# Even layer in parity order: tokens stay sorted by parity up to the heads' outputs

## The chip, the cores and the metric

One Trainium2 chip; the program runs on one of its cores. The metric is the device time of one execution in microseconds (us), as the median over several runs. The profiled execution is a run of its own, and its trace gives the start and length of every instruction on TensorE (PE for matmuls, PEld for its weight loads), VectorE (DVE), ScalarE (ACT), GpSimd (POOL) and on the DMA queues.

## The reference, cut to what matters

A two-layer encoder over 256 tokens of width 2048. The even layer projects the normalised input to two groups of heads: A, eight heads of dilated window attention with three dilations each, and B, four heads of differential attention. The dilations are 1, 4 and 16, so keys of the two wider groups always have the parity of the query's token.

```python
def even_mixer(y, w_in, w_out, ...):
    proj = jnp.einsum("bsd,de->bse", y, w_in)
    pa = proj[..., :a_cols].reshape(b, s, A_GROUPS, 3, A_HEADS, HEAD_DIM)
    for gi, (window, dilation) in enumerate(((128, 1), (512, 4), (2048, 16))):
        o, lse = dilated_window_attention(pa[:, :, gi, 0], pa[:, :, gi, 1], pa[:, :, gi, 2], cols, window, dilation)
    out_a = jnp.sum(softmax(lses) * outs)
    o_b = differential_attention(q_b, k_b, v_b, t5_table[:, 24:], lam)
    o_b = rmsnorm(o_b, subln) * (1.0 - lambda_init)
    return jnp.einsum("bse,ed->bsd", concat(out_a, out_b), w_out)

def reference(x, ...):
    for layer in range(2):
        h = h + (even_mixer if layer % 2 == 0 else odd_mixer)(rmsnorm(h, ln_mix[layer]), ...)
        h = h + conv_ffn(rmsnorm(h, ln_ffn[layer]), ...)
    return rmsnorm(h, ln_final)
```

## The kernel before

All weights stream from HBM in units of 128 x 1024 fp32 (`wunit`, DMAs on SP's queue). Each unit is split into two fp32r parts: ScalarE casts the high part (`wh`), VectorE subtracts to get the low part (`wl`). Activations are held the same way, as two parts of 128 features x 256 tokens (`yT`). A product of two such numbers takes three partial products.

Two kinds of projection exist. `gemm_b` makes features x tokens (used for q and k): the weights are the stationary operand and all 256 tokens stream past. `gemm_a` makes tokens x features (used for V and for output projections): 128 tokens of `yT` are the stationary operand and 512 columns of weights stream past. `gemm_a` with 16 feature tiles has 8 units, and a unit has 2 feature tiles x 2 token blocks x 3 partial products = 12 matmuls. In the A heads, the V products of the two wider dilations (g = 1 and 2) pass `strided=True`: their token blocks are all even and all odd tokens, read out of natural order with a step of two.

The row factor 1 / rms of the layer norm isn't applied to `yT`; it is applied to the products. `row_factor` gives `rstd` (tokens on partitions). `row_broadcast` spreads it to `R` (tokens along the free axis): VectorE copies each half to a 128 x 128 tile `rb`, two TensorE transposes put them into a PSUM tile, VectorE copies that to `R`. Then two more TensorE transposes of `R`, read with a step of two, give `rstd_par`: the factors of the even and of the odd tokens on partitions (lines 390 to 401). `v_tiles` scales a V product by `rstd` or `rstd_par` while it copies it out of PSUM: ScalarE the high part, VectorE then the low part.

The PSUM pool has four tiles with the tag `gm`; each `gemm_a` takes two. So the third `gemm_a` can start only when `v_tiles` has read the first. The first V product of a head group runs ahead of `row_factor`, the second too (`v_ps`).

For q and k, `halves` multiplies by `Rq` or `R` and writes the tokens in parity order and reversed (q of A), in parity order (k of the wider groups), reversed (q of B) or plainly. `a_local` and `b_logits` add the bias to the logits through `bias_view`. `a_values` and the transposes of B's probabilities bring the tokens back to natural order.

The order of work is that of the program's text, with a small list of pending work (`later`, `tick`): softmax, transposes and value products of one head run some projections later. A scheduler then sets each engine's own order; engines run theirs strictly in order and wait for one another by semaphores.

Of the kernel before, what the change touches and what calls it, by code (L numbers as in the profile page):

```python
# [54 lines left out]
def trunk_kernel(ctx: ExitStack, tc, a, out):  # L58
# [13 lines left out]
    def nm(s):  # L72
        uid[0] += 1
        return f"{s}_{uid[0]}"
# [61 lines left out]
        tick()  # L136
        return ps

    def a_unit(ps, src, u, act, nk, strided=False, parts=1):
        last = 2 * u + 2 == nk  # L140
        a_products(ps, wunit(src[u], parts), u, act, nk, strided,
                   [(t, k) for t in range(2) for k in range(2)] if last else
                   [(t, k) for k in range(2) for t in range(2)])

    def a_products(ps, w, u, act, nk, strided, order):
        wh, wl = w
        for t, k in order:
            kt = u * 2 + k
            sl = slice(k * 512, (k + 1) * 512)
            if strided:  # L150
                ah, al = (act[kt][:, x, :].rearrange("p (j r) -> p r j", r=2)[:, t, :] for x in range(2))
            else:
                ah, al = (act[kt][:, x, t * P:(t + 1) * P] for x in range(2))
            T.matmul(ps[t], ah, wh[:, sl], start=(kt == 0), stop=False)  # L154
            T.matmul(ps[t], ah, wl[:, sl], start=False, stop=False)  # L155
            T.matmul(ps[t], al, wh[:, sl], start=False, stop=(kt == nk - 1))  # L156

    def gemm_a(src, act, nk, strided=False, hooks={}, first=1):

        ps = [tps("gm", 4), tps("gm", 4)]  # L160
        for u in range(nk // 2):
            if u in hooks:
                hooks[u]()
            a_unit(ps, src, u, act, nk, strided, parts=1 if u else first)
            if u % 2 == 1:
                tick()
        return ps

    def natural(ap):
        return ap.rearrange("p (a b) -> p a b", b=2)  # L170
# [9 lines left out]
    def halves(ps, r, order=None):  # L180

        t0 = tmp.tile([P, SEQ], F32, name=nm("t0"), tag="t0")
        S.copy(t0, ps[:, 0, :])  # L183
        V.tensor_tensor(t0, t0, ps[:, 1, :], op=ALU.add)  # L184
        t2 = tmp.tile([P, SEQ], F32, name=nm("t2"), tag="t2")
        if order in (parity, parity_rev):
            V.tensor_tensor(order(t2), natural(t0), natural(r), op=ALU.mult)
        else:
            V.tensor_tensor(order(t2) if order else t2, t0, r, op=ALU.mult)
        return t2  # L190

    def split(dst_h, dst_l, src):
# [47 lines left out]
    def row_factor():  # L240
        ss = tmp.tile([P, 2], F32, name=nm("ss"), tag="ss")
        V.tensor_reduce(ss, ssq_now[0], axis=AX.X, op=ALU.add)
        return rsqrt_mean(ss, D, "rstd", const)

    def row_broadcast(rstd):

        ps = tps("tp", 2)
        for t in range(2):
            b = tmp.tile([P, P], F32, name=nm("rb"), tag="rb")
            V.tensor_copy(b, rstd[:, t:t + 1].to_broadcast([P, P]))  # L250
            T.transpose(ps[:, t * P:(t + 1) * P], b, ident)
        r = const.tile([P, SEQ], F32, name=nm("R"), tag="R", bufs=1)
        V.tensor_copy(r, ps[:, 0:SEQ])
        return r

    def query_factor(R):
# [51 lines left out]
    def logits(q, k):  # L308
        ps = two(tps("s", 2))
        for t in range(2):  # L310
            qh = q[:, 0, t * P:(t + 1) * P]
            ql = q[:, 1, t * P:(t + 1) * P]
            T.matmul(ps[:, t, :], qh, k[:, 0, :], start=True, stop=False)  # L313
            T.matmul(ps[:, t, :], qh, k[:, 1, :], start=False, stop=False)  # L314
            T.matmul(ps[:, t, :], ql, k[:, 0, :], start=False, stop=True)  # L315
        return ps

    def bias_view(b, step):

# [58 lines left out]
    def x_rows(c):  # L378
# [8 lines left out]
    bmask = load("bmask", (28, NREL), pool=tmp, tag="ry", eng=nc.sync)  # L387
    onehot2 = load("onehot2", (32, 256), pool=tmp, tag="rx", eng=nc.sync)
    bmask2 = load("bmask2", (16, 256), pool=tmp, tag="ry", eng=nc.sync)
    v_ps.append(gemm_a(a["eva_v"][1], yT, KT, strided=True,  # L390
                       hooks={u: lambda u=u: x_rows(u) for u in range(4)}))
    for c in range(4):
        squares(c)
    rstd = row_factor()
    R = row_broadcast(rstd)
    Rq = query_factor(R)
    rstd_par = const.tile([P, 2], F32, name="rstd_par")
    ps = two(tps("tp", 2))
    for t in range(2):
        T.transpose(ps[:, t, 0:P], R.rearrange("p (j r) -> p r j", r=2)[:, t, :], ident)  # L400
    V.tensor_copy(rstd_par, ps[:, :, 0])

    rel = dram.tile([28, NREL + 1], F32, name="rel")
# [13 lines left out]
    def new_sc():  # L417
        return att.tile([P, 2, 512], F32, name=nm("sc"), tag="sc", bufs=1)

    def a_bias(hd, g):  # L420
        if g:
            b = att.tile([P, P], F32, name=nm("bias2"), tag="bias2", bufs=2)
            G.dma_start(b, bass.AP(tensor=rel2.tensor, offset=rel2.offset + ((g - 1) * 8 + hd) * 256,
                                   ap=[[1, P], [1, P]]))
            return b
        b = att.tile([P, 384], F32, name=nm("bias"), tag="bias", bufs=2)
        G.dma_start(b[:, 0:257], bass.AP(tensor=rel.tensor, offset=rel.offset + hd * (NREL + 1),
                                         ap=[[2, P], [1, 257]]))
        return b

    def a_local(q, k, b, sc):
        sc.append(new_sc())
        sc = sc[0]
        V.tensor_tensor(sc[:, :, 0:SEQ], logits(q, k), bias_view(b, 1), op=ALU.add)

    def a_strided(g, q, k, b, sc):

# [45 lines left out]
    def a_head(hd, vg):  # L483
        sc = []
        for g in range(3):
            b = a_bias(hd, g)
            q = qk_tile(a["eva_qk"][hd * 6 + 2 * g], yT, Rq, parity_rev, 2 * g)
            k = qk_tile(a["eva_qk"][hd * 6 + 2 * g + 1], yT, R, parity if g else None, 2 * g + 1)
            if g == 0:
                later(2, lambda q=q, k=k, b=b: a_local(q, k, b, sc))  # L490
            else:
                later(2, lambda g=g, q=q, k=k, b=b: a_strided(g, q, k, b, sc))

        def soft():
            softmax(sc[0])
            later(2, lambda: a_transposes(sc[0], hd, vg), 1)
        later(2, soft)

    for hh in range(2):
        vg = []  # L500
        for g in range(3):
            ps = v_ps.pop(0) if v_ps else gemm_a(a["eva_v"][hh * 3 + g], yT, KT, strided=(g > 0))
            if hh and g == 0:
                flush()
            vg.append(v_tiles(ps, rstd_par if g else rstd, range(8 + 4 * g, 12 + 4 * g)))
        for hd in range(hh * 4, hh * 4 + 4):
            a_head(hd, vg)

# [15 lines left out]
    def b_logits(m, q, k, sc, bias):  # L524
        if m == 0:
            sc.append(new_sc())
        V.tensor_tensor(sc[0][:, :, m * SEQ:(m + 1) * SEQ], logits(q, k), bias_view(bias, P), op=ALU.add)

    def b_softmax(hd, sc, vt):
        w = sc[0].rearrange("p t (m k) -> p t m k", m=2)  # L530
# [14 lines left out]
        later(2, lambda: b_transposes(hd, w, vt), 1)  # L545

    def b_transposes(hd, w, vt):
        pt = transposed_probs(w[:, 0, 0, :], w[:, 1, 0, :], rev)
        later(1, lambda: b_values(hd, pt, vt), 0)

    def b_values(hd, pt, vt):
# [19 lines left out]
    def b_finish(hd, o):  # L571
        ps = two(tps("tp", 2))
        for f in range(2):
            for t in range(2):
                T.transpose(ps[:, f, t * P:(t + 1) * P], o[:, t, f * P:(f + 1) * P], ident)
            y = new_act("mix", 8 + 2 * hd + f)
            split_scaled(y[:, 0, :], y[:, 1, :], ps[:, f, :], sub_gain[:, f:f + 1])
            mix[8 + 2 * hd + f] = y

    for pair in range(2):  # L580
        vt = v_tiles(gemm_a(a["evb_v"][pair], yT, KT), rstd, range(20 - 4 * pair, 24 - 4 * pair))
        for hd in (2 * pair, 2 * pair + 1):
            bias = att.tile([P, 384], F32, name=nm("bias"), tag="bias", bufs=2)
            G.dma_start(bias, bass.AP(tensor=rel.tensor, offset=rel.offset + (24 + hd) * (NREL + 1),
                                      ap=[[1, P], [1, 384]]))
            sc = []
            for m in range(2):
                q = qk_tile(a["evb_qk"][hd * 4 + m], yT, Rq, rev, 2 * m)
                k = qk_tile(a["evb_qk"][hd * 4 + 2 + m], yT, R, None, 2 * m + 1)
                later(2, lambda m=m, q=q, k=k, sc=sc, bias=bias: b_logits(m, q, k, sc, bias))  # L590
            later(2, lambda hd=hd, sc=sc, vt=vt: b_softmax(hd, sc, vt))
# [187 lines left out]
    def finish_all(src, act, y):  # L779
# [12 lines left out]
        kept = [(u, wunit(src[3][u])) for u in range(nu - AHEAD, nu)]  # L792
        for t in range(2):
            for u, w in kept:
                a_products(ps, w, u, act, HALF_F, False, [(t, 0), (t, 1)])
            finish_rows(t, ps[t])

    ffn(1, yT, None, last=True)
# [50 lines left out]
def _arrays(i):  # L849
    i = {k: np.asarray(v) for k, v in i.items()}  # L850
    r = {}
    r["x"] = i["x"].reshape(SEQ, D)
    r["xT"] = i["x"].reshape(SEQ, 8, 2, P).transpose(1, 3, 2, 0).reshape(8, P, 2 * SEQ)
    r["ln"] = np.stack([i["ln_mix"], i["ln_ffn"]]).reshape(4, KT, P).transpose(2, 0, 1)
    r["lnf"] = i["ln_final"]
    r["t5"] = i["t5_table"]
# [47 lines left out]
```

## Time and profile before

| | |
|---|---|
| median of 3 runs | 2485.79 us (2485.61 to 2485.87) |
| the profiled execution | 2485.5 us |
| its span, first to last instruction | 2483.7 us |
| TensorE matmuls busy | 2472.6 us |
| VectorE busy | 1671.2 us |
| ScalarE busy | 1227.8 us |
| DMA, mean rate | 187 GB/s |

The span leaves 1.8 us of the execution outside of it. Busy time of TensorE counts a matmul from its issue to its modelled end, so consecutive matmuls overlap; the step between their starts tells the pace. The A heads run until some 440 us, the B heads until some 585 us, the even layer's output projection follows, then the first FFN and the odd layer.

### The profile page before, as it was taken

The numbers are of one execution on the slowest core, as the hardware profiler recorded it, in microseconds if no ns is written. First come the engines' busy times: TensorE is split into PE (matmuls) and PEld (weight loads), VectorE is DVE, ScalarE is ACT, GpSimd is POOL, SyncE is SP. The second block draws the span as 40 slices with busy tenths as digits, with TensorE's granted clock in tenths as the row PEclk, the third lists the DMA queues.
The fourth block names the chain that finished last, engine by engine and source line by source line (L and its number), as shares of the span: only waits on it lengthen the run. The fifth ranks groups of instructions, "written<-read, shape, count | busy, mean of one in ns | idle before, by whom it ended". The sixth has DMA issues, their size and how long they took to land.

```text
span 2483.7 us, 34336 instructions
## 1 busy us (share of the span) xinstructions
PE 2472.6 (100%) x13115; PEld 2124.2 (86%) x13115; DVE 1671.2 (67%) x2454; ACT 1227.8 (49%) x1853; POOL 45.7 (2%) x71
## 2 busy tenths in 40 slices
PE   9999999999999999999999999999999999999998
PEld 7888888888888888888888888888888888888887
DVE  6677577676577775477775568765777755777754
ACT  6454445465554443344444457545544433444443
POOL 0000000001000000000000000100000000000000
PEclk9999999999999999999999999999999999999999
DMA  8655555556555555566655555765565655655654
GB/s 290 198 170 180 182 180 182 181 181 176 175 188 188 187 188 193 193 189 189 190 185 190 187 186 164 174 175 180 186 192 187 188 191 193 192 188 188 191 188 144
DMA packets 129951, 463.86 MB, mean 187 GB/s; under 512 B 15216, under 2 KB 15340, under 8 KB 129786
## 3 DMA queue, kind: packets, MB, share of 16 engines
q1 hardware_dynamic: 127018, 455.31, 57.1%
q0 software_dynamic: 2624, 6.32, 2.3%
q8 instruction: 102, 1.67, 0.3%
q14 instruction: 63, 0.52, 0.1%
q10 hardware_dynamic: 144, 0.03, 0.0%
HBM read 459.44 MB, written 2.17 MB: 186 GB/s over the span
## 4 chain that ended last, share of the span: by engine, by line
PE 99%; DMA 0%; DVE 0%; ACT 0%; SPq 0%; issue 0%; DVEq 0%; ACTq 0%
PE gm L126 38%; PE gm L129 20%; PE gm L155 13%; PE gm L154 13%; PE gm L156 13%; PE tp L330 0%; PE tp L237 0%; PE s L313 0%; PE s L315 0%; PE s L314 0%; DMA raw<-in_eva_v 0%; PE s L474 0%; PE s L443 0%; PE s L467 0%; PE s L342 0%; PE s L341 0%
## 5 line engine op out<-in xcount | busy, mean ns | idle before, releaser
L194 DVE TENSOR_TENSOR wl<-raw,wh 128x1024 fp32r<-128x1024 f32 (+1 forms) x857 | 1049.0, 1225 | 723.8 <-ACT wh L193 719.4
L193 ACT CAST wh<-raw 128x1024 fp32r<-128x1024 f32 (+1 forms) x857 | 898.6, 1049 | 1146.4 <-issue 501.8
L126 PE MATMUL gm<-yT,wh 128*128 128x512 f32 x4096 | 1029.1, 393 | 0.0
L126 PEld LDWEIGHTS gm<-yT,wh 128*128 128x128 f32 x4096 | 736.5, 189 | 132.6 <-DVE yT L200 0.7
L129 PEld LDWEIGHTS gm<-yT,wl 128*128 128x128 f32 x4096 | 558.7, 190 | 39.8
L129 PE MATMUL gm<-yT,wl 128*128 128x256 f32 x4096 | 571.2, 282 | 0.0
L154 PE MATMUL gm<-wh,prod 128*128 128x512 f32 x704 | 274.5, 390 | 0.0
L156 PE MATMUL gm<-wh,prod 128*128 128x512 f32 x704 | 274.3, 390 | 0.0
L155 PE MATMUL gm<-wl,prod 128*128 128x512 f32 x704 | 274.0, 389 | 0.0
L155 PE MATMUL gm<-wl,yT 128*128 128x512 f32 x416 | 163.4, 393 | 0.5 <-DVE wl L194 0.5
L154 PE MATMUL gm<-wh,yT 128*128 128x512 f32 x416 | 163.3, 395 | 0.5 <-ACT wh L193 0.5
L156 PE MATMUL gm<-wh,yT 128*128 128x512 f32 x416 | 163.0, 392 | 0.0
L156 PEld LDWEIGHTS gm<-wh,prod 128*128 128x128 f32 x704 | 132.2, 188 | 27.4
L155 PEld LDWEIGHTS gm<-wl,prod 128*128 128x128 f32 x704 | 132.2, 188 | 27.1
L154 PEld LDWEIGHTS gm<-wh,prod 128*128 128x128 f32 x704 | 132.2, 188 | 27.0
L184 DVE TENSOR_TENSOR t<-t,gm 128x256 f32<-128x256 f32 x256 | 105.9, 414 | 0.0
L154 PE MATMUL gm<-wh,mix 128*128 128x512 f32 x256 | 101.0, 394 | 0.0
L155 PE MATMUL gm<-wl,mix 128*128 128x512 f32 x256 | 100.4, 392 | 0.0
L156 PE MATMUL gm<-wh,mix 128*128 128x512 f32 x256 | 100.3, 393 | 0.0
L155 PEld LDWEIGHTS gm<-wl,yT 128*128 128x128 f32 x416 | 78.9, 190 | 17.3 <-DVE wl L194 1.4
L154 PEld LDWEIGHTS gm<-wh,yT 128*128 128x128 f32 x416 | 78.6, 190 | 17.5 <-ACT wh L193 1.4
L183 ACT COPY t<-gm 128x256 f32<-128x256 f32 x256 | 92.9, 363 | 0.0
(206 smaller groups left out, 1506.7 us busy)
## 6 DMA issues: line engine op xcount, KB each, us to landing
raw<-in_up SPq DMA_DIRECT2D x352, 512.0 KB, 4.3
raw<-in_down SPq DMA_DIRECT2D x176, 512.0 KB, 3.4
raw<-in_eva_qk SPq DMA_DIRECT2D x96, 512.0 KB, 3.5
raw<-in_eva_v SPq DMA_DIRECT2D x47, 512.0 KB, 3.5
raw<-in_evb_qk SPq DMA_DIRECT2D x32, 512.0 KB, 3.3
raw<-in_ev_out SPq DMA_DIRECT2D x32, 512.0 KB, 3.5
raw<-in_od_qk SPq DMA_DIRECT2D x32, 512.0 KB, 3.5
raw<-in_od_out SPq DMA_DIRECT2D x32, 512.0 KB, 3.4
```

Source lines behind the costliest of these rows:

```text
L126: T.matmul(flat, wh[:, sl], y.rearrange("p a b -> p (a b)"), start=(u == 0 and k == 0), stop=False)
L129: T.matmul(ps[:, 1, :], wl[:, sl], y[:, 0, :], start=False, stop=(u * 8 + k == KT - 1))
L154: T.matmul(ps[t], ah, wh[:, sl], start=(kt == 0), stop=False)
L155: T.matmul(ps[t], ah, wl[:, sl], start=False, stop=False)
L156: T.matmul(ps[t], al, wh[:, sl], start=False, stop=(kt == nk - 1))
L183: S.copy(t0, ps[:, 0, :])
L184: V.tensor_tensor(t0, t0, ps[:, 1, :], op=ALU.add)
L193: S.copy(dst_h, src)
L194: V.tensor_tensor(dst_l, src, dst_h.bitcast(F32), op=ALU.subtract)
```

## The change

The tokens of the even layer are put in parity order (all even tokens, then all odd ones) on the host, in `xT`. Thus `yT` is in parity order, and every `gemm_a` reads plain runs of 128 tokens; the `strided` form goes. `row_broadcast` writes the first layer's `R` in parity order, `rstd_par` is transposed from plain halves of it, and all V products of the even layer are scaled by `rstd_par` (before, A's g = 0 and both of B were scaled by `rstd`). q is only reversed and k is written plainly. The biases of A's g = 0 and of B come from one loader, `row_bias` (rows that step by two, 257 columns), and are added through the stepped view `parity_bias`. B's outputs go back to natural order where they leave PSUM in `b_finish`. The weights, the products and their number stay.

```diff
-    def a_products(ps, w, u, act, nk, strided, order):
+    def a_products(ps, w, u, act, nk, order):
...
-            if strided:
-                ah, al = (act[kt][:, x, :].rearrange("p (j r) -> p r j", r=2)[:, t, :] for x in range(2))
-            else:
-                ah, al = (act[kt][:, x, t * P:(t + 1) * P] for x in range(2))
+            ah, al = (act[kt][:, x, t * P:(t + 1) * P] for x in range(2))
...
-        if order in (parity, parity_rev):
-            V.tensor_tensor(order(t2), natural(t0), natural(r), op=ALU.mult)
-        else:
-            V.tensor_tensor(order(t2) if order else t2, t0, r, op=ALU.mult)
+        V.tensor_tensor(order(t2) if order else t2, t0, r, op=ALU.mult)
...
-        V.tensor_copy(r, ps[:, 0:SEQ])
+        if by_parity:
+            V.tensor_copy(parity(r), natural(ps[:, 0:SEQ]))
+        else:
+            V.tensor_copy(r, ps[:, 0:SEQ])
...
+    def parity_bias(b):
+
+        return bass.AP(tensor=b.tensor, offset=b.offset, ap=[list(b.ap[0]), [1, 2], [1, 2], [2, P]])
+
+    def by_parity(ap):
+        return ap.rearrange("p t (b a) -> p t b a", b=2)
...
-    R = row_broadcast(rstd)
+    R = row_broadcast(row_factor(), by_parity=True)
...
-        T.transpose(ps[:, t, 0:P], R.rearrange("p (j r) -> p r j", r=2)[:, t, :], ident)
+        T.transpose(ps[:, t, 0:P], R[:, t * P:(t + 1) * P], ident)
...
-        V.tensor_tensor(sc[:, :, 0:SEQ], logits(q, k), bias_view(b, 1), op=ALU.add)
+        V.tensor_tensor(by_parity(sc[:, :, 0:SEQ]), by_parity(logits(q, k)), parity_bias(b), op=ALU.add)
...
-            q = qk_tile(a["eva_qk"][hd * 6 + 2 * g], yT, Rq, parity_rev, 2 * g)
-            k = qk_tile(a["eva_qk"][hd * 6 + 2 * g + 1], yT, R, parity if g else None, 2 * g + 1)
+            q = qk_tile(a["eva_qk"][hd * 6 + 2 * g], yT, Rq, rev, 2 * g)
+            k = qk_tile(a["eva_qk"][hd * 6 + 2 * g + 1], yT, R, None, 2 * g + 1)
...
-            vg.append(v_tiles(ps, rstd_par if g else rstd, range(8 + 4 * g, 12 + 4 * g)))
+            vg.append(v_tiles(ps, rstd_par, range(8 + 4 * g, 12 + 4 * g)))
...
-            split_scaled(y[:, 0, :], y[:, 1, :], ps[:, f, :], sub_gain[:, f:f + 1])
+            split_scaled(natural(y[:, 0, :]), natural(y[:, 1, :]), parity_rev(ps[:, f, :]), sub_gain[:, f:f + 1])
...
-            G.dma_start(bias, bass.AP(tensor=rel.tensor, offset=rel.offset + (24 + hd) * (NREL + 1),
-                                      ap=[[1, P], [1, 384]]))
+            bias = row_bias(24 + hd)
...
-    r["xT"] = i["x"].reshape(SEQ, 8, 2, P).transpose(1, 3, 2, 0).reshape(8, P, 2 * SEQ)
+    order = np.concatenate([np.arange(0, SEQ, 2), np.arange(1, SEQ, 2)])
+    r["xT"] = i["x"].reshape(SEQ, 8, 2, P)[order].transpose(1, 3, 2, 0).reshape(8, P, 2 * SEQ)
```

The engines' orders change in one place beside the views. TensorE before, where the second V product of the A heads (gm_321, gm_322) ends and the third (gm_539, gm_540) begins; `rb` are the copies of `rstd`, both transposes write the PSUM tag `tp`:

```order
L156 MATMUL gm_322<-wh_455,yT_290 128x512
L251 MATMUL tp_495<-ident,rb_496 128x128
L251 MATMUL tp_495<-ident,rb_499 128x128
L154 MATMUL gm_539<-wh_543,yT_102 128x512
L155 MATMUL gm_539<-wl_544,yT_102 128x512
L156 MATMUL gm_539<-wh_543,yT_102 128x512
L154 MATMUL gm_540<-wh_543,yT_102 128x512
L400 MATMUL tp_507<-ident,R_502 128x128 x2
L155 MATMUL gm_540<-wl_544,yT_102 128x512
```

TensorE in the changed kernel, at the same place (its line numbers are those of the changed file):

```order
L154 MATMUL gm_322<-wh_455,yT_290 128x512
L246 MATMUL tp_495<-ident,rb_496 128x128
L246 MATMUL tp_495<-ident,rb_499 128x128
L404 MATMUL tp_507<-ident,R_502 128x128 x2
L152 MATMUL gm_539<-wh_543,yT_102 128x512
L153 MATMUL gm_539<-wl_544,yT_102 128x512
L154 MATMUL gm_539<-wh_543,yT_102 128x512
L152 MATMUL gm_539<-wh_543,yT_105 128x512
L152 MATMUL gm_540<-wh_543,yT_102 128x512
```

The transposes of R moved ahead of the third V product's first matmul; before, four of its matmuls stood between the two pairs of transposes.

VectorE before, around the same transposes (the scaled copies of the first V product, gm_98 and gm_99, stand much earlier, right behind `wl_402`):

```order
L200 SCALAR_TENSOR_TENSOR v_524<-gm_98,rstd_493,v_523 128x512
L200 SCALAR_TENSOR_TENSOR v_528<-gm_99,rstd_493,v_527 128x512
...
L413 TENSOR_TENSOR vals_518<-s_519,bmask_319 16x256
L253 COPY R_502<-tp_495 128x256
L258 TENSOR_SCALAR Rq_504<-R_502 128x256
L194 TENSOR_TENSOR wl_598<-raw_595,wh_597 128x1024
L401 COPY rstd_par<-tp_507 128x2
L200 SCALAR_TENSOR_TENSOR v_532<-gm_321,rstd_par,v_531 128x512
L200 SCALAR_TENSOR_TENSOR v_536<-gm_322,rstd_par,v_535 128x512
```

VectorE in the changed kernel:

```order
L417 TENSOR_TENSOR vals_518<-s_519,bmask_319 16x256
L249 COPY R_502<-tp_495 128x128x2
L256 TENSOR_SCALAR Rq_504<-R_502 128x256
L189 TENSOR_TENSOR wl_598<-raw_595,wh_597 128x1024
L405 COPY rstd_par<-tp_507 128x2
L195 SCALAR_TENSOR_TENSOR v_524<-gm_98,rstd_par,v_523 128x512
L195 SCALAR_TENSOR_TENSOR v_528<-gm_99,rstd_par,v_527 128x512
L195 SCALAR_TENSOR_TENSOR v_532<-gm_321,rstd_par,v_531 128x512
L195 SCALAR_TENSOR_TENSOR v_536<-gm_322,rstd_par,v_535 128x512
```

The scaled copies of the first V product moved from ahead of the third product's weight splits to behind the copy to `rstd_par`. ScalarE's halves of them (v_523, v_527) moved alike, behind the cast of `wh_597`.

## Rows read from the trace of the kernel before

**Rows 1.** The page: busy time of TensorE (share of the span, instructions), and the shares of the chain that ended last, by engine.
```profile
PE 2472.6 (100%) x13115; PEld 2124.2 (86%) x13115; DVE 1671.2 (67%) x2454; ACT 1227.8 (49%) x1853; POOL 45.7 (2%) x71
PE 99%; DMA 0%; DVE 0%; ACT 0%; SPq 0%; issue 0%; DVEq 0%; ACTq 0%
```

**Rows 2.** The waits of TensorE over the whole span: who waited for whom, us in total, times, longest.
```profile
PE s L368 <- DVE zeros L365: 1.5, 1, 1.5
PE gm L155 <- DVE wl L194: 0.5, 1, 0.5
PE gm L154 <- ACT wh L193: 0.5, 1, 0.5
```

**Rows 3.** Busy time of the engines in three stretches, here their sum (60 to 620 us), and the first stretch: its length, busy us of each engine (instructions), granted clock, DMA share, GB/s.
```profile
60.00:200.00 140.00, 140.00 (x802) 123.13 (x801) 96.28 (x140) 69.75 (x105) 4.36 (x9) 1.00 0.60 183
...
sum 560.00, PE 560.00 PEld 487.98 DVE 384.39 ACT 290.11 POOL 24.15; mean PE 186.67 PEld 162.66 DVE 128.13 ACT 96.70 POOL 8.05
```

**Rows 4.** Timeline of TensorE, first V product (g = 0): start us, length us, what. The first and the last of 52 matmuls in a row.
```profile
17.43 0.39 PE L156 MATMUL gm<-wh,yT 128*128 128x512 f32 x1
...
28.99 0.39 PE L156 MATMUL gm<-wh,yT 128*128 128x512 f32 x1
```

**Rows 5.** Timeline of TensorE, V products that read every second token: the first and the last of 73 matmuls of the third V product, then the first and the last of 46 of one in the second half of the heads.
```profile
58.00 0.39 PE L156 MATMUL gm<-wh,yT 128*128 128x512 f32 x1
...
74.80 0.39 PE L156 MATMUL gm<-wh,yT 128*128 128x512 f32 x1
279.73 0.39 PE L156 MATMUL gm<-wh,yT 128*128 128x512 f32 x1
...
290.23 0.39 PE L156 MATMUL gm<-wh,yT 128*128 128x512 f32 x1
```

**Rows 6.** Timeline of ScalarE: the scaled copies of the first V product, and of the second.
```profile
36.81 1.26 ACT L197 ACTIVATE v<-gm,rstd 128x512 fp32r<-128x512 f32 x2
...
56.13 1.27 ACT L197 ACTIVATE v<-gm,rstd_par 128x512 fp32r<-128x512 f32 x2 [1.37 <-DVE rstd_par L401]
```

**Rows 7.** Timeline of VectorE: its part of the first V product's scaled copies, then the stretch around the transposes.
```profile
38.08 1.40 DVE L200 SCALAR_TENSOR_TENSOR v<-gm,rstd,v 128x512 fp32r<-128x512 f32 x2
...
53.82 0.41 DVE L413 TENSOR_TENSOR vals<-s,bmask 16x256 f32<-16x256 f32 x1 [0.60 <-PE tp L251]
54.16 0.40 DVE L253 COPY R<-tp 128x256 f32<-128x256 f32 x1
54.60 0.30 DVE L258 TENSOR_SCALAR Rq<-R 128x256 f32<-128x256 f32 x1
54.81 1.22 DVE L194 TENSOR_TENSOR wl<-raw,wh 128x1024 fp32r<-128x1024 f32 x1
55.95 0.15 DVE L401 COPY rstd_par<-tp 128x2 f32<-128x2 f32 x1
56.86 1.41 DVE L200 SCALAR_TENSOR_TENSOR v<-gm,rstd_par,v 128x512 fp32r<-128x512 f32 x2 [0.76 <-ACT v L197]
```

**Rows 8.** Timeline of TensorE around the two pairs of transposes.
```profile
53.28 0.40 PE L156 MATMUL gm<-wh,yT 128*128 128x512 f32 x1
53.51 0.38 PE L251 MATMUL tp<-ident,rb 128*128 128x128 f32 x2
53.65 0.48 PE L154 MATMUL gm<-wh,yT 128*128 128x512 f32 x1
53.97 0.39 PE L155 MATMUL gm<-wl,yT 128*128 128x512 f32 x1
...
54.43 0.40 PE L154 MATMUL gm<-wh,yT 128*128 128x512 f32 x1
54.67 0.46 PE L400 MATMUL tp<-ident,R 128*128 128x128 f32 x2
54.88 0.48 PE L155 MATMUL gm<-wl,yT 128*128 128x512 f32 x1
55.20 0.39 PE L156 MATMUL gm<-wh,yT 128*128 128x512 f32 x1
```

**Rows 9.** Groups of instructions by line and shape: how many, busy us in all, mean ns of one, then idle time before them.
```profile
L184 DVE TENSOR_TENSOR t<-t,gm 128x256 f32<-128x256 f32 x256 | 105.9, 414 | 0.0
L189 DVE TENSOR_TENSOR t<-t,R 128x256 f32<-128x256 f32 x200 | 84.7, 424 | 6.1
L187 DVE TENSOR_TENSOR t<-t,Rq 128x256 f32<-128x256 f32 x24 | 15.2, 635 | 0.8
L187 DVE TENSOR_TENSOR t<-t,R 128x256 f32<-128x256 f32 x16 | 10.2, 636 | 0.3
L434 DVE TENSOR_TENSOR sc<-s,bias 128x512 f32<-128x512 f32 x8 | 5.5, 682 | 0.0
L478 DVE TENSOR_TENSOR t<-t,s 128x256 f32<-128x256 f32 x8 | 3.4, 420 | 3.9 <-ACT t L477 3.9
L253 DVE COPY R<-tp 128x256 f32<-128x256 f32 x4 | 1.7, 418 | 0.3
...
L477 ACT COPY t<-s 128x256 f32<-128x256 f32 x8 | 3.0, 373 | 10.0 <-PE s L475 9.9
```

**Rows 10.** Timeline of the program's start: TensorE's first nine matmuls, which read zeros, its first V product, and one pair of VectorE's split and the matmul that waits for it.
```profile
1.49 4.18 PE L368 MATMUL s<-zeros 128*128 128x512 f32 x9 [1.49 <-DVE zeros L365]
...
5.50 0.69 PE L154 MATMUL gm<-wh,yT 128*128 128x512 f32 x2
...
9.21 1.23 DVE L194 TENSOR_TENSOR wl<-raw,wh 128x1024 fp32r<-128x1024 f32 x1 [1.20 <-ACT wh L193]
...
10.49 0.50 PE L155 MATMUL gm<-wl,yT 128*128 128x512 f32 x1 [0.53 <-DVE wl L194]
```

More of the change, by code (lines that the diff above doesn't have):

```diff
@@ L137, in gemm_b, with a_unit @@
         return ps
-    def a_unit(ps, src, u, act, nk, strided=False, parts=1):
+    def a_unit(ps, src, u, act, nk, parts=1):
         last = 2 * u + 2 == nk
-        a_products(ps, wunit(src[u], parts), u, act, nk, strided,
+        a_products(ps, wunit(src[u], parts), u, act, nk,
                    [(t, k) for t in range(2) for k in range(2)] if last else
                    [(t, k) for k in range(2) for t in range(2)])
-    def a_products(ps, w, u, act, nk, strided, order):
+    def a_products(ps, w, u, act, nk, order):
         wh, wl = w
@@ L156, in a_products, with gemm_a @@
             T.matmul(ps[t], al, wh[:, sl], start=False, stop=(kt == nk - 1))
-    def gemm_a(src, act, nk, strided=False, hooks={}, first=1):
+    def gemm_a(src, act, nk, hooks={}, first=1):
         ps = [tps("gm", 4), tps("gm", 4)]
@@ L163, in gemm_a @@
                 hooks[u]()
-            a_unit(ps, src, u, act, nk, strided, parts=1 if u else first)
+            a_unit(ps, src, u, act, nk, parts=1 if u else first)
             if u % 2 == 1:
@@ L243, in row_factor, with row_broadcast @@
         return rsqrt_mean(ss, D, "rstd", const)
-    def row_broadcast(rstd):
+    def row_broadcast(rstd, by_parity=False):
         ps = tps("tp", 2)
@@ L389, in trunk_kernel @@
     bmask2 = load("bmask2", (16, 256), pool=tmp, tag="ry", eng=nc.sync)
-    v_ps.append(gemm_a(a["eva_v"][1], yT, KT, strided=True,
+    v_ps.append(gemm_a(a["eva_v"][1], yT, KT,
                        hooks={u: lambda u=u: x_rows(u) for u in range(4)}))
@@ L393, in trunk_kernel @@
         squares(c)
-    rstd = row_factor()
-    R = row_broadcast(rstd)
+    R = row_broadcast(row_factor(), by_parity=True)
     Rq = query_factor(R)
@@ L418, in new_sc, with row_bias @@
         return att.tile([P, 2, 512], F32, name=nm("sc"), tag="sc", bufs=1)
+    def row_bias(row):
+        b = att.tile([P, 384], F32, name=nm("bias"), tag="bias", bufs=2)
+        G.dma_start(b[:, 0:257], bass.AP(tensor=rel.tensor, offset=rel.offset + row * (NREL + 1),
+                                         ap=[[2, P], [1, 257]]))
+        return b
     def a_bias(hd, g):
@@ L425, in a_bias @@
             return b
[L426 to L429, printed above, removed]
+        return row_bias(hd)
     def a_local(q, k, b, sc):
@@ L501, in trunk_kernel @@
         for g in range(3):
-            ps = v_ps.pop(0) if v_ps else gemm_a(a["eva_v"][hh * 3 + g], yT, KT, strided=(g > 0))
+            ps = v_ps.pop(0) if v_ps else gemm_a(a["eva_v"][hh * 3 + g], yT, KT)
             if hh and g == 0:
                 flush()
-            vg.append(v_tiles(ps, rstd_par if g else rstd, range(8 + 4 * g, 12 + 4 * g)))
+            vg.append(v_tiles(ps, rstd_par, range(8 + 4 * g, 12 + 4 * g)))
         for hd in range(hh * 4, hh * 4 + 4):
@@ L526, in b_logits @@
             sc.append(new_sc())
-        V.tensor_tensor(sc[0][:, :, m * SEQ:(m + 1) * SEQ], logits(q, k), bias_view(bias, P), op=ALU.add)
+        V.tensor_tensor(by_parity(sc[0][:, :, m * SEQ:(m + 1) * SEQ]), by_parity(logits(q, k)), parity_bias(bias),
+                        op=ALU.add)
     def b_softmax(hd, sc, vt):
@@ L547, in b_transposes @@
     def b_transposes(hd, w, vt):
-        pt = transposed_probs(w[:, 0, 0, :], w[:, 1, 0, :], rev)
+        pt = transposed_probs(w[:, 0, 0, :], w[:, 1, 0, :])
         later(1, lambda: b_values(hd, pt, vt), 0)
@@ L576, in b_finish @@
             y = new_act("mix", 8 + 2 * hd + f)
-            split_scaled(y[:, 0, :], y[:, 1, :], ps[:, f, :], sub_gain[:, f:f + 1])
+            split_scaled(natural(y[:, 0, :]), natural(y[:, 1, :]), parity_rev(ps[:, f, :]), sub_gain[:, f:f + 1])
             mix[8 + 2 * hd + f] = y
     for pair in range(2):
-        vt = v_tiles(gemm_a(a["evb_v"][pair], yT, KT), rstd, range(20 - 4 * pair, 24 - 4 * pair))
+        vt = v_tiles(gemm_a(a["evb_v"][pair], yT, KT), rstd_par, range(20 - 4 * pair, 24 - 4 * pair))
         for hd in (2 * pair, 2 * pair + 1):
-            bias = att.tile([P, 384], F32, name=nm("bias"), tag="bias", bufs=2)
-            G.dma_start(bias, bass.AP(tensor=rel.tensor, offset=rel.offset + (24 + hd) * (NREL + 1),
-                                      ap=[[1, P], [1, 384]]))
+            bias = row_bias(24 + hd)
             sc = []
@@ L794, in finish_all @@
             for u, w in kept:
-                a_products(ps, w, u, act, HALF_F, False, [(t, 0), (t, 1)])
+                a_products(ps, w, u, act, HALF_F, [(t, 0), (t, 1)])
             finish_rows(t, ps[t])
```

## The prediction

> **What bounds the kernel now.** Read the busy shares and the chain first: TensorE is busy for 2472.6 of 2483.7 us and carries 99% of the chain that ended last [rows 1]. Then its waits: three in the whole run, 2.5 us together [rows 2]; the later two end by 10.49 us, so afterwards no matmul waits for another engine's result. The time is therefore TensorE's own instruction stream, end to end. Only two things can move it: a different pace of that stream, or a new wait in it. VectorE is busy for 384 of the 560 us that follow in the even layer's heads [rows 3]; what it saves or spends there counts only if it makes TensorE wait.
>
> So the next thing to read is the pace, as the step between starts of consecutive 512-column matmuls. In the first V product, whose stationary operand is a run of 128 tokens, the start moves from 17.43 to 28.99 us in 51 matmuls: 0.2267 us each [rows 4]. In the third V product, whose stationary operand is every second token, it moves from 58.00 to 74.80 in 72: 0.2333 each; in a V product of the second half of the heads from 279.73 to 290.23 in 45: 0.2333 again [rows 5]. The two forms differ in the stationary operand's step alone, so the step costs 6.67 ns a matmul.
>
> **What the change removes from TensorE.** Four of the six V products of the A heads read every second token. Each has 8 units of 12 matmuls: 4 x 96 = 384 matmuls. At 6.67 ns, 384 x 6.67 ns = **2.56 us** less. One of the four lies ahead of the place discussed next, three behind it.
>
> The Trainium skill's page "SBUF — State Buffer", in its note on cachelines under "Door 1: The DMA port swizzle", says that a read may step over up to four 4-byte elements at full bandwidth. The step here is two. By that note the old read is free already, this gain is 0, and the sum below would be that of the second rival. The rows differ from the note: 0.2333 against 0.2267, so I take the measured gain.
>
> **What the change adds.** Before, the first V product is scaled by `rstd`, ready early: ScalarE takes its two halves at 36.81 us, VectorE at 38.08 [rows 6, 7], 15 us before its PSUM tiles are wanted again. Now it is scaled by `rstd_par`, which comes out of four small transposes on TensorE that stand behind the second V product. PSUM has four `gm` tiles; the first two products fill them, so the third (gm_539, gm_540) cannot start until the first is scaled and read. The order shows it: before, the third product's first four matmuls fill the time between the two pairs of transposes; now both pairs come first and gm_539 behind them. I follow the chain with T0 = start of the first pair (53.51 in the old trace [rows 8]):
>
> - VectorE's `vals2` (it takes over a buffer that the first pair reads) starts 0.31 after T0, the copy to R 0.34 later (53.82, 54.16 [rows 7]): +0.65.
> - The copy to R now writes pairs 128 elements apart. No row shows that copy. Its bounds: 0.42 us as it is [rows 9], or 0.64, as the q multiplies that write through the same view take (L187 0.635, against 0.424 for the plain L189). I take 0.64, since it is the writing view that the slow rows share: +0.22. The copy ends at +1.29.
> - The second pair of transposes starts at +1.34 (a result of VectorE is picked up 0.05 us after its end: 9.21 + 1.23 = 10.44, then 10.49 [rows 10]). The first pair reached VectorE 0.31 after its start, so this one is there by about +1.7.
> - VectorE meanwhile does Rq and one weight split `wl_598` (1.22 us), which still stands ahead of the `rstd_par` copy. That copy started at 55.95, T0 + 2.44; with the 0.22 it is +2.66. So the split, not the transposes, sets it.
> - ScalarE starts the scaled copy 0.18 later (56.13 [rows 6]), +2.84; VectorE starts its half 0.73 after ScalarE (56.86 [rows 7]), +3.57, and takes 0.75 (two pipelined: 1.41): +4.32.
> - TensorE starts gm_539 at **+4.37**. gm_540 is wanted four matmuls (0.9 us) later and its scaling ends 0.66 after the first, so it costs nothing more.
>
> Before, gm_539 started at 53.65, T0 + 0.14. The delay is 4.23. From it comes off what the second pair cost while the stream ran: from 54.43 to 55.20, two matmuls took 0.77 in place of 0.47 [rows 8], 0.30 that now lies inside the wait. New wait: **3.93 us**. With 0.42 for the copy it is 3.71; if the first matmul after the wait costs as much more as the step behind the transposes (0.32 against 0.23), some 4.0. What is queued behind the waiting instructions: on ScalarE three more scaled copies and the cast of the fifth unit, due some 4 x 2.7 us after the restart; on VectorE the like. Neither is late.
>
> **What is hidden.** The q and k multiplies stop writing pairs: 40 x (0.635 - 0.424) = 8.4 us less on VectorE [rows 9]. TensorE waits for none of them, so 0 is taken; were VectorE the bound, it would be 8.4. The 16 bias additions of the A and B heads read every second bias through a four-part view: between nothing and the factor of 1.5 that L187 shows over L189, 16 x 0.34 = 5.5 us; I take nothing, since only a large writing step is slow in these rows. The eight B output splits read PSUM through the reversed parity view and write plainly. L477 and L478 do the same at 0.373 and 0.420, beside 0.414 for the plain L184: nothing. Bounds by the factor 1.5 on these too add some 2 us. All of it lies under the 560 - 384 = 176 us that VectorE has free [rows 3]. The bias loads get smaller and stay off the path.
>
> **Sum.** Against the profiled execution's own 2485.5: - 2.56 + 3.93 = +1.4, so 2486.9. The median of the runs is 0.3 above that execution: **2487.2 us**.
>
> **Rivals.**
> 1. *The clock falls in the wait.* TensorE is all but idle for some 4 us, with two small transposes in it. The column of granted clock reads 1.00 in the stretches of [rows 3], and the 0.2267 us steps are the 2.4 GHz level. At the program's start nine 512-column matmuls take from 1.49 to 5.50 [rows 10], 0.446 each, the 1.2 GHz level, after an idle engine. A second start like it costs 9 x (0.446 - 0.227) = 2.0 us: **2489.2**. For it: nowhere after 11 us does the old trace have such a pause. Against it: two waits of 0.5 us [rows 2] did not bring the slow pace back. The Trainium skill ("TensorE: Matmul & The Clock Gate", "What's actually happening") says the same in general: idle brings the slow level, sustained matmuls lift it; whether this pause is enough no row shows. *On the slower side:* the loss grows by 0.22 us a matmul while the low level lasts, so with 1.4 already lost, slower by over 0.2% (5.0 us) needs over 16 matmuls at the low level, nearly twice what the start shows. That is its point of decision; 17 of them give 2490.9.
> 2. *The pace stays 0.2333.* Then only the wait is left: **2489.7**. The two paces [rows 4, 5] speak against it.
> 3. *No wait comes*, because the chain ends before TensorE reaches gm_539. Then only the gain is left: 2485.8 - 2.6 = **2483.2**. Against it: each step above is a row, and even without the split ahead of `rstd_par` (0.9 us) the wait stays above 2.56.
> 4. *VectorE falls behind in the heads* through the new views: the bounds above, 7.5 us of 176 free, don't reach TensorE. For that one addition (0.682, L434) would have to grow several times over. Sixteen waits like the 0.5 us one that TensorE had for VectorE at the start [rows 2] would give 2487.2 + 8 = **2495**.
>
> **How the numbers follow.** What a measurement of this kernel tells from no change is about 0.2%, 5.0 us: 2480.8 to 2490.8. Chances: forecast 0.57; clock 0.25, of it 0.05 past its point of decision; pace 0.06; no wait 0.06; VectorE behind 0.03; something faster by over 5 us that no row shows 0.03. Hence faster 0.03, slower 0.05 + 0.03 = 0.08, within 0.89. By the copy and the restart the forecast itself lies between 2486.9 and 2487.4. Below it the range reaches to the wait without the split ahead of `rstd_par` (0.9 less, 2486.0), above it to the clock at its price from the start and to the lost pace, and it takes 0.4 on either side for the spread between runs and what I read off rounded rows: **2485.6 to 2490.1**, which leaves 0.17 out.
>
> **What would show it.** In the new trace: V products all at 0.2267; one TensorE wait of about 4 us near 53 us, put down to VectorE's scaling of v, with the copy to R at about 0.64; no other wait past 11 us; q and k multiplies at 0.42; the granted clock 1.00 behind the wait and steps of 0.2267 there. I am wrong if those steps are near 0.43 (rival 1), if the V products stay at 0.2333, if the wait is under 2.5 us, or if TensorE waits in the heads.

## The result, and the profile after

| | before | changed |
|---|---|---|
| median of 22 runs | 2485.61 us (2484.91 to 2486.01) | 2489.09 us (2487.92 to 2490.56) |
| ratio to before | | 1.0014, 95% interval 1.0009 to 1.0020 |
| span of the profiled execution | 2483.7 us | 2487.0 us |

The time is 3.5 us longer, inside the forecast range and inside the 0.2% that was called no change. The interval excludes 1, so the loss is real, though small. But the time is not the forecast case of 2487.2 us: it lies on rival 1, the clock, at 2489.2. Rival 2, the pace of 0.2333, stands close by at 2489.7, so the time alone does not decide between them; the trace does.

The waits of TensorE in the changed kernel, over the whole span (columns as in [rows 2]):

```profile
PE gm L152 <- DVE v L195: 2.6, 1, 2.6
PE s L373 <- DVE zeros L370: 1.5, 1, 1.5
PE tp L404 <- DVE R L249: 0.9, 1, 0.9
PE gm L153 <- DVE wl L189: 0.5, 1, 0.5
PE gm L152 <- ACT wh L188: 0.4, 1, 0.4
```

The three short waits of [rows 2] are still there. Two are new: 0.9 us for the copy to R, 2.6 us for the first V product's scaling. After them there is none: no wait came up in the heads.

TensorE's timeline around these two waits, which answers to [rows 8] (start us, length us, what, and the idle time before it):

```profile
52.76 0.40 PE L154 MATMUL gm<-wh,yT 128*128 128x512 f32 x1
52.99 0.38 PE L246 MATMUL tp<-ident,rb 128*128 128x128 f32 x2
54.29 0.44 PE L404 MATMUL tp<-ident,R 128*128 128x128 f32 x2 [0.91 <-DVE R L249]
57.37 0.51 PE L152 MATMUL gm<-wh,yT 128*128 128x512 f32 x1 [2.64 <-DVE v L195]
57.71 0.59 PE L153 MATMUL gm<-wl,yT 128*128 128x512 f32 x1
58.10 0.63 PE L154 MATMUL gm<-wh,yT 128*128 128x512 f32 x1
58.53 1.05 PE L152 MATMUL gm<-wh,yT 128*128 128x512 f32 x2
...
61.09 0.43 PE L152 MATMUL gm<-wh,yT 128*128 128x512 f32 x1
61.36 0.40 PE L153 MATMUL gm<-wl,yT 128*128 128x512 f32 x1
...
65.02 0.39 PE L154 MATMUL gm<-wh,yT 128*128 128x512 f32 x1
...
69.78 0.39 PE L154 MATMUL gm<-wh,yT 128*128 128x512 f32 x1
```

From T0 = 52.99 the third V product starts at 57.37, +4.38; the forecast was +4.37. Then look at the steps: from 58.10 to 61.09 seven of them took 2.99 us, 0.43 us a matmul, against 0.2267 between 65.02 and 69.78 (21 steps). That last pace, of a V product that stood at 0.2333 before, also rules out rival 2. Ten steps from 57.37 to 61.36 took 3.99 us; at 0.2267 they would take 2.27, and the first step is 0.11 longer (57.37 to 57.71), as it also is in the experiment below that keeps the engine busy (57.39 to 57.73). The rest, 1.6 us, is the clock. The busy times and the granted clock of short stretches say the same (stretch, its length, then busy us of PE, PEld, DVE, ACT, POOL with instructions, granted clock, DMA share, GB/s):

```profile
52.00:57.00 5.00, 1.81 (x10) 1.08 (x8) 3.68 (x7) 2.20 (x4) 0.85 (x2) 1.00 0.60 197
57.00:58.00 1.00, 0.63 (x2) 0.59 (x3) 1.00 (x3) 1.00 (x3) 0.76 (x2) 0.87 0.86 279
58.00:59.00 1.00, 1.00 (x4) 0.71 (x4) 1.00 (x2) 0.27 (x1) 0.00 (x0) 0.50 0.82 234
...
61.00:62.00 1.00, 1.00 (x5) 0.77 (x4) 0.00 (x0) 0.00 (x0) 0.00 (x0) 0.93 0.00 0
```

The granted clock is 1.00 (2.4 GHz) on the mean through the pause, 0.50 (1.2 GHz) behind the restart, and 1.00 again. The means of 0.87 and 0.93 put the fall near 57.7 and the rise near 61.1 us. Between 52.99 and its restart at 57.37 TensorE had done nothing but four small transposes.

VectorE and ScalarE in between, answering to [rows 6, 7]:

```profile
53.30 0.41 DVE L417 TENSOR_TENSOR vals<-s,bmask 16x256 f32<-16x256 f32 x1 [0.53 <-PE tp L246]
53.64 0.59 DVE L249 COPY R<-tp 128x256 f32<-128x256 f32 x1
...
54.53 1.21 DVE L189 TENSOR_TENSOR wl<-raw,wh 128x1024 fp32r<-128x1024 f32 x1
55.66 0.14 DVE L405 COPY rstd_par<-tp 128x2 f32<-128x2 f32 x1
55.84 2.43 ACT L192 ACTIVATE v<-gm,rstd_par 128x512 fp32r<-128x512 f32 x4 [1.61 <-DVE rstd_par L405]
56.56 2.72 DVE L195 SCALAR_TENSOR_TENSOR v<-gm,rstd_par,v 128x512 fp32r<-128x512 f32 x4 [0.76 <-ACT v L192]
```

This is the forecast chain, step by step: the `rstd_par` copy at T0 + 2.67 (forecast 2.66), ScalarE at + 2.85 (2.84), VectorE at + 3.57 (3.57). The copy to R took 0.59, between its bounds of 0.42 and 0.64.

The groups that answer to [rows 9], and the sum of the three stretches of [rows 3]:

```profile
L184 DVE TENSOR_TENSOR t<-t,Rq 128x256 f32<-128x256 f32 x40 | 16.9, 423 | 1.1
L441 DVE TENSOR_TENSOR sc<-s,bias 128x512 f32<-128x512 f32 x8 | 5.4, 680 | 0.0
...
sum 560.00, PE 560.00 PEld 487.82 DVE 375.96 ACT 289.94 POOL 23.37; mean PE 186.67 PEld 162.61 DVE 125.32 ACT 96.65 POOL 7.79
```

The q multiplies fell from 0.635 to 0.423 us, the bias additions through the stepped view stayed at 0.68, and VectorE is busy for 376.0 us in place of 384.4: 8.4 us less, with TensorE at 560 of 560 both times. The stretches don't hold quite the same work, as the changed kernel runs some 4 us behind in them; over the whole run VectorE's busy time fell from 1671.2 to 1662.4 us, by 8.8. So VectorE's saving is real and worth nothing here.

### The profile page after: what moved, and what is told of

Same layout as the page of the kernel before. It is cut to its first block, busy times and chain, and to the rows that moved or that the text cites. A ratio compares the mean times of both kernels' runs of the same rounds, so it can differ in the third digit from the quotient of the medians.

```text
span 2487.0 us, 34336 instructions
## 1 busy us (share of the span) xinstructions
PE 2472.5 (99%) x13115; PEld 2123.6 (85%) x13115; DVE 1662.4 (67%) x2454; ACT 1227.7 (49%) x1853; POOL 45.3 (2%) x71
## 4 chain that ended last, share of the span: by engine, by line
PE 99%; DVE 0%; DMA 0%; ACT 0%; SPq 0%; issue 0%; DVEq 0%; ACTq 0%
PE gm L127 38%; PE gm L130 20%; PE gm L153 13%; PE gm L152 13%; PE gm L154 13%; PE tp L335 0%; PE tp L232 0%; PE s L311 0%; PE s L313 0%; PE s L312 0%; DMA raw<-in_eva_v 0%; PE s L481 0%; PE s L450 0%; PE s L474 0%; PE s L347 0%; PE s L346 0%
## 5 line engine op out<-in xcount | busy, mean ns | idle before, releaser
L184 DVE TENSOR_TENSOR t<-t,R 128x256 f32<-128x256 f32 x216 | 91.4, 424 | 6.4
```

## Experiments

Theory: three terms make the difference. Reading runs of 128 tokens saves 2.6 us, the new wait costs 3.9, and the clock's fall behind it another 1.9. Rivals: the step costs nothing and the wait is shorter than it looks; the loss beyond the forecast lies in the changed views in the heads. Each experiment's time is the median of 11 runs. The kernel before, run beside them, stood at 2485.75 us (beside the last three at 2485.61), so 0.1 us between experiments tells nothing.

**The step alone.** The kernel before, with one edit:

```diff
-            if strided:
-                ah, al = (act[kt][:, x, :].rearrange("p (j r) -> p r j", r=2)[:, t, :] for x in range(2))
-            else:
-                ah, al = (act[kt][:, x, t * P:(t + 1) * P] for x in range(2))
+            ah, al = (act[kt][:, x, t * P:(t + 1) * P] for x in range(2))
```

> The kernel before with one thing changed: the V products of the wider groups read runs of 128 tokens of yT in place of every second token. So the A heads pair keys with values of other tokens; the work and the order stay. Theory (the step of two costs 6.67 ns a matmul): 384 steps of 0.2267 in place of 0.2333 us, 2485.6 - 2.6 = 2483.0 us. Rival (the step is free, and the slower pace of those products comes from something else in their place in the program): 2485.6 us, steps of 0.2333.

Measured: 2483.32 us against 2485.75 for the kernel before (ratio 0.9992, 0.9983 to 1.0001). The first and the last of 73 matmuls of the third V product, which answer to [rows 5]:

```profile
58.15 0.39 PE L153 MATMUL gm<-wh,yT 128*128 128x512 f32 x1
...
74.47 0.39 PE L153 MATMUL gm<-wh,yT 128*128 128x512 f32 x1
```

The pace is 16.32 / 72 = 0.2267 in the same place where it was 0.2333, so it is the stationary operand's step that makes the difference, and the gain of 2.4 us agrees with 2.6. The interval reaches just past 1; that the next run, with the same reads, gives the same time supports the gain. Two of the 11 runs here (2485.27 and 2485.61), and two of the next run's (2485.16 and 2485.89), are 1.9 to 2.7 us longer than the median; none of the 33 runs of the kernel before is so far off. None of these four executions was traced, so the cause stays open.

**No wait.** The changed kernel with the row factors made inside the second V product (`early(u)` also calls `x_rows` for u below 4):

```diff
+        elif u == 5:
+            for c in range(4):
+                squares(c)
+            facs["R"] = row_broadcast(row_factor(), by_parity=True)
+            facs["Rq"] = query_factor(facs["R"])
+        elif u == 6:
+            ps = two(tps("tp", 2))
+            for t in range(2):
+                T.transpose(ps[:, t, 0:P], facs["R"][:, t * P:(t + 1) * P], ident)
+            V.tensor_copy(rstd_par, ps[:, :, 0])
...
-                       hooks={u: lambda u=u: x_rows(u) for u in range(4)}))
+                       hooks={u: lambda u=u: early(u) for u in range(8)}))
```

> The changed kernel, with the row factors made earlier: squares, row_factor and the copy to R stand ahead of unit 5 of the second V product, the transposes to rstd_par ahead of unit 6, so that the first V product is scaled before TensorE reaches the third. Theory (the reads of 128-token runs give 384 x 6.67 ns = 2.6 us, the wait and the clock's fall behind it take 5.5 to 6): no TensorE wait past 11 us, granted clock 1.00 throughout, 2485.6 - 2.6 = 2483.0 us. Rival (the wait is all of the loss, the runs of 128 tokens give nothing): 2485.6 us, as before. Rival (something else in the changed views costs time in the heads): 2484 us or more, with TensorE waits after 80 us.

Measured: 2483.23 us, ratio 0.9991 (0.9983 to 1.0). Its waits:

```profile
PE s L373 <- DVE zeros L370: 1.5, 1, 1.5
PE gm L152 <- ACT wh L188: 0.7, 1, 0.7
PE gm L153 <- DVE wl L189: 0.5, 1, 0.5
```

Only the start's waits are left, and the granted clock reads 1.00 from 51 to 66 us. The kernel has all of the change's views, and its time is that of the step alone within 0.1 us: the q and k multiplies, the biases and B's outputs together neither give nor take anything that shows. It is 5.9 us below the changed one.

**The wait alone.** The kernel before, where the first V product's factor is made to depend on `rstd_par`:

```diff
+    rstd_late = const.tile([P, 2], F32, name="rstd_late")
+    V.scalar_tensor_tensor(rstd_late, rstd_par, 0.0, rstd, op0=ALU.mult, op1=ALU.add)
...
-            vg.append(v_tiles(ps, rstd_par if g else rstd, range(8 + 4 * g, 12 + 4 * g)))
+            vg.append(v_tiles(ps, rstd_par if g else rstd_late, range(8 + 4 * g, 12 + 4 * g)))
```

> The kernel before, with one thing added: the first V product is scaled by a copy of rstd that VectorE makes out of rstd_par (times zero) and rstd, so it has to wait for rstd_par as in the changed kernel. The strided reads and all views stay. Theory (the wait alone costs time, and the clock falls behind it): a wait of some 4.4 us net (one scaled copy of the second product now stands ahead of the first one's), and 1.7 us at the low clock: 2491.7 us, steps of 0.427 us behind the wait. Rival (the wait without the clock): 2490.0 us. Rival (the wait is not what made the changed kernel slower): 2485.8 us.

Measured: 2491.08 us, ratio 1.0020 (1.0012 to 1.0029), 5.3 us above the kernel before; 6.1 were expected with the clock's fall, 4.4 without. Its timeline of TensorE, one short stretch, and VectorE's first scaled copy behind the wait:

```profile
54.06 0.38 PE L251 MATMUL tp<-ident,rb 128*128 128x128 f32 x2
55.16 0.50 PE L400 MATMUL tp<-ident,R 128*128 128x128 f32 x2 [0.73 <-DVE R L253]
58.20 0.51 PE L154 MATMUL gm<-wh,yT 128*128 128x512 f32 x1 [2.53 <-DVE v L200]
...
60.24 0.63 PE L156 MATMUL gm<-wh,yT 128*128 128x512 f32 x1
60.66 0.63 PE L155 MATMUL gm<-wl,yT 128*128 128x512 f32 x1
59.00:60.00 1.00, 1.00 (x4) 0.80 (x3) 1.00 (x2) 0.10 (x1) 0.65 (x2) 0.53 0.42 107
57.40 0.75 DVE L200 SCALAR_TENSOR_TENSOR v<-gm,rstd_par,v 128x512 fp32r<-128x512 f32 x1 [0.56 <-ACT v L197]
```

The third product starts at T0 + 4.14, where I expected some 4.8: VectorE's first scaled copy, one of the second product's, ends at 57.40 + 0.75 = 58.15, and TensorE goes on 0.05 later. So the copy that I had put in the chain stands behind it, and the third product seems to take over a tile of the second product. The chain here gives 4.14 - 0.14 - 0.30 = 3.7 net, so 2489.5 without the clock, and the 1.6 that remain are the clock. The slow steps (0.42 us from 60.24 to 60.66) begin later behind the restart than in the changed kernel: the mean granted clock of 0.53 between 59 and 60 us puts the fall near 59.1, some 0.9 us behind it. Two of its 11 runs lie near 2489 (2488.59, 2489.36), the others between 2490.5 and 2492.2.

**The wait, with TensorE busy.** The changed kernel with twelve unread matmuls between the transposes of R and the third V product:

```diff
-        T.transpose(ps[:, t, 0:P], R[:, t * P:(t + 1) * P], ident)
+        tc.keep_in_program_order(T.transpose(ps[:, t, 0:P], R[:, t * P:(t + 1) * P], ident))
...
+    fill = tps("tp", 2)
+    for _ in range(12):
+        tc.keep_in_program_order(T.matmul(fill, yT[0][:, 0, 0:P], yT[1].rearrange("p a b -> p (a b)"),
+                                          start=True, stop=True))
```

> The changed kernel with twelve 512-column matmuls, whose results nobody reads, put into the wait between the transposes to rstd_par and the third V product (12 x 0.227 = 2.7 us of a wait of 2.9). The third product can start no earlier than in the changed kernel, but TensorE is busy until then. Theory (the changed kernel's extra over the forecast is the clock's fall in the pause): granted clock 1.00 behind the wait, steps of 0.227 us, 2485.6 - 2.6 + 4.0 = 2487.0 us, and less spread between runs than the changed kernel's 2487.9 to 2490.6. Rival (the extra is something else): 2488.7 to 2489.1 us, like the changed kernel.

Measured: 2487.22 us (2487.00 to 2488.13). TensorE's timeline and one short stretch:

```profile
54.30 0.44 PE L404 MATMUL tp<-ident,R 128*128 128x128 f32 x2 [0.91 <-DVE R L249]
54.50 2.99 PE L408 MATMUL tp<-yT,yT 128*128 128x512 f32 x12
57.39 0.50 PE L152 MATMUL gm<-wh,yT 128*128 128x512 f32 x1
57.73 0.40 PE L153 MATMUL gm<-wl,yT 128*128 128x512 f32 x1
57.96 0.39 PE L154 MATMUL gm<-wh,yT 128*128 128x512 f32 x1
...
59.00:60.00 1.00, 1.00 (x6) 0.82 (x5) 0.31 (x1) 0.00 (x0) 0.02 (x1) 1.00 0.78 57
```

This is the run that separates the terms. The third product starts at 57.39, as in the changed kernel (57.37), so the wait is paid in full; but the engine was busy, the granted clock stays at 1.00 and the steps at 0.23. Work that nobody reads makes the kernel 1.9 us faster, and its runs (2487.00 to 2488.13) hardly overlap the changed kernel's (2487.92 to 2490.56). It is also the forecast's own case: 2487.22 for 2487.2. Against the run without the wait, the wait alone costs 2487.22 - 2483.23 = 4.0 us (forecast 3.93); against the changed kernel, the clock costs 2489.09 - 2487.22 = 1.9 (2.0 in rival 1).

**A shorter pause, twice.** First the changed kernel with only three of those matmuls:

```diff
-    for _ in range(12):
+    for _ in range(3):
```

> The changed kernel with three of the twelve unread matmuls in the wait (0.7 of 2.9 us, right behind the transposes to rstd_par), so that a pause of some 2.1 us is left ahead of the third V product. Theory (the length of the last pause decides): the clock falls in fewer runs or not at all, 2487.2 to 2488.5 us. Rival (any pause of this kind brings the fall): 2489.1 us, steps of 0.427 behind the wait.

Measured: 2489.07 us, ratio 1.0014 (1.0005 to 1.0022). TensorE's restart and two matmuls behind it:

```profile
57.36 0.50 PE L152 MATMUL gm<-wh,yT 128*128 128x512 f32 x1 [1.96 <-DVE v L195]
...
59.24 0.63 PE L153 MATMUL gm<-wl,yT 128*128 128x512 f32 x1
59.67 0.63 PE L154 MATMUL gm<-wh,yT 128*128 128x512 f32 x1
```

One of the 11 runs is at 2486.90, the others lie between 2488.26 and 2490.10; the steps of the profiled execution (2488.92) are 0.43 from 59.24 on. So, as far as the times tell, a last pause of 2.0 us still brings the fall nearly each time; the theory that it would be rare fell.

Then the changed kernel with the copy to `rstd_par` on ScalarE:

```diff
-    V.tensor_copy(rstd_par, ps[:, :, 0])
+    S.copy(rstd_par, ps[:, :, 0])
```

> The changed kernel with the copy to rstd_par on ScalarE in place of VectorE, so that it no longer stands behind the weight split. Theory (the split sets when rstd_par is there, not the transposes): the first scaled copy on ScalarE starts near 54.9 us in place of 55.84, VectorE's half follows the split at 55.8, TensorE restarts 0.8 us earlier, near 56.5. If the clock still falls: 2489.1 - 0.8 = 2488.3 us; if the shorter pause keeps the clock: 2486.4 us. Rival (the transposes or the copy to R set it): TensorE restarts at 57.4 as in the changed kernel, 2489.1 us.

Measured: 2487.92 us, ratio 1.0007 (0.9998 to 1.0016). Its scaled copies and TensorE's restart:

```profile
54.34 0.16 ACT L405 COPY rstd_par<-tp 128x2 f32<-128x2 f32 x1 [0.52 <-PE tp L404]
54.53 2.43 ACT L192 ACTIVATE v<-gm,rstd_par 128x512 fp32r<-128x512 f32 x4
52.57 0.38 PE L246 MATMUL tp<-ident,rb 128*128 128x128 f32 x2
56.06 0.80 PE L152 MATMUL gm<-wh,yT 128*128 128x512 f32 x1 [1.75 <-DVE v L195]
```

TensorE restarts at T0 + 3.49 in place of 4.38, 0.9 us earlier: the weight split ahead of the copy did set the chain. The 11 runs stand in two groups, four between 2486.08 and 2486.44 and seven between 2487.80 and 2488.74: with the clock kept and with its fall, as the two expected times of 2486.4 and 2488.3 have it. That the groups are these two states is read from the times; the profiled execution, which is of the upper group (2488.74), shows the fall.

**A step of four.** The kernel before, with the strided products reading every fourth element across the high and the low part:

```diff
-                ah, al = (act[kt][:, x, :].rearrange("p (j r) -> p r j", r=2)[:, t, :] for x in range(2))
+                ah, al = (act[kt].rearrange("p a b -> p (a b)").rearrange("p (j r) -> p r j", r=4)[:, t, :]
+                          for x in range(2))
```

> The kernel before, where the V products of the wider groups read yT with a step of four elements, across its high and low part, in place of two (so they take wrong tokens and parts; the work and the order stay). Theory A (the cost grows with the distance, 6.67 ns per element of extra step): 20 ns a matmul, steps of 0.2467 us, 2483.2 + 384 x 0.020 = 2490.9 us. Theory B (any step costs the same 6.67 ns): steps of 0.2333, 2485.7 us, as before. Rival (up to four elements are free): 2483.2 us, which the run of the step alone already speaks against.

Measured: 2486.89 us, ratio 1.0005 (0.9996 to 1.0013). The weight loads of the third V product between 58 and 75 us, the same matmul's group at the step of two (kernel before) and of four (busy us, mean ns of one, idle before), then the first and the last of 73 matmuls at a step of four:

```profile
L154 PEld LDWEIGHTS gm<-wh,yT 128*128 128x128 f32 x25 | 4.8, 193 | 1.0
```
```profile
L155 PEld LDWEIGHTS gm<-wh,yT 128*128 128x128 f32 x25 | 7.7, 309 | 0.0
...
58.00 0.40 PE L157 MATMUL gm<-wh,yT 128*128 128x512 f32 x1
...
74.92 0.40 PE L157 MATMUL gm<-wh,yT 128*128 128x512 f32 x1
```

The pace is 16.92 / 72 = 0.2350. Both theories miss: a second doubling of the step adds only 1.7 ns to the pace, while the load itself goes from 193 to 309 ns. On 384 matmuls 1.7 ns is 0.6 us, half of the 1.3 us by which this run is longer than the kernel before. Part of the rest lies in the first steps behind other work: behind the two pairs of transposes they take 0.44 and 0.42 us, where [rows 8] have 0.32, and these 0.10 to 0.12 are about what the load grew by. That elsewhere the matmul ahead of a load hides most of it would fit, but no run here shows it, and what sets the 6.7 ns stays open.

## Why the prediction was right, and where it was not

- *TensorE's stream is the bound; only its pace or a new wait counts.* Held. VectorE lost 8.4 us of work in the heads (8.8 in the whole run), as worked out, and the run without the wait equals the step alone within 0.1 us.
- *384 x 6.67 ns = 2.56 us less.* Held: 2.4 in the step alone, 2.5 without the wait. The note on cachelines in the Trainium skill's page "SBUF — State Buffer" ("Door 1: The DMA port swizzle") allows a step of up to four 4-byte elements at full bandwidth; here two cost 6.7 ns a matmul and four cost 8.3. The measurement decides against it for the stationary operands here.
- *A wait of 3.93 us.* Held in place, size and cause: the restart came at + 4.38 for + 4.37, and the wait with TensorE kept busy costs 4.0. In the trace it stands as two waits, 0.9 and 2.6 us, with the second pair of transposes between them. The upper end of the forecast's own span is added up a little high: with 0.09 for the restart it comes to 2487.3, not 2487.4.
- *The likeliest case.* This step failed. I gave the clock's fall 0.25 against 0.57 for its staying up, because two waits of 0.5 us had not brought the slow pace. That was no evidence about 4.4 us with four small transposes in them, over eight times as long. The mechanism, its place and its price (2.0 for 1.9) stood in rival 1. That the price came so close is luck in part: it was taken from nine matmuls at the start, where the profiled execution here has seven full slow steps and parts of two, and over 2487.22 the 22 runs lose between 0.7 and 3.3 us. The level at the start was read from the pace of 0.446 alone, as the old trace's column of granted clock reads 1.00 there too; here column and pace agree, 0.50 and 0.43. The Trainium skill's "TensorE: Matmul & The Clock Gate" ("What's actually happening") says in general what then happened: here the granted clock went to 0.50 behind the pause. No run of the changed kernel comes down to 2487.2, the lowest of 22 is 2487.92; by that, the fall seems to come in practically every run.
- *The point of decision on the slower side*, 16 matmuls at the low clock, was not reached: seven full slow steps stand in the trace (58.10 to 61.09), and parts of two at their ends. That is one execution, of 2488.79 us. The longest of the 22 runs, 2490.56, lies 3.3 us above 2487.22; at 0.2 us a matmul that is an estimated 16 or 17 slow ones, so this run came close to that point.
- *The range and the call of no change* held, with the time near the upper end. The range held because it was drawn to take in rival 1, not because the case given 0.57 came about.

## What to carry to other kernels

When one engine's stream is the bound, go through what a change makes that stream wait for, before counting what it saves elsewhere: here one scale factor that comes out later turned a gain of 2.5 us into a loss of 3.5, and making it two units earlier brings the gain back. Here a pause of some microseconds on TensorE had to be priced twice, as its own length (4.0 us) and as the slow matmuls behind it (1.9), and unread matmuls in the pause saved the second price. The 8.8 us of work taken off VectorE, which TensorE did not wait for, were worth nothing.

## What the runs showed of the hardware that I had not expected

- The clock fell behind pauses that were short and broken: with 0.9 and 2.0 us idle, and two small transposes and three full matmuls between them, it still fell in ten of 11 runs, as far as their times tell; with 0.9 and 1.75 us, and the transposes between, in about seven of 11. With 0.9 us alone, in the run that filled the rest of the wait, it stayed.
- The fall did not keep one distance from the restart: by the mean granted clock of short stretches it lies 0.4 us behind it in the changed kernel, 0.9 with the wait alone, some 1.5 with three unread matmuls, and ahead of it, in the pause, with the copy on ScalarE (0.63 between 55 and 56 us, restart at 56.06).
- A shorter pause did not make the slow stretch shorter in the execution that was traced: with the copy on ScalarE the clock is at 0.50 from 56 to 61 us at least, longer than the 57.7 to 61.1 of the changed kernel, with TensorE at work throughout:

```profile
56.00:57.00 1.00, 0.94 (x2) 0.83 (x3) 1.00 (x3) 0.96 (x2) 0.00 (x0) 0.50 0.67 174
60.00:61.00 1.00, 1.00 (x4) 0.74 (x3) 0.00 (x0) 0.00 (x0) 0.00 (x0) 0.50 0.08 8
```

- A stationary operand read with a step cost pace on these fp32 data, though the loads overlap the matmuls in the trace: 0.2267 us a matmul at a step of one, 0.2333 at two, 0.2350 at four.
